# Arithmetic moved from GpSimd to VectorE, a hand-set order in the routing, and norms finished on the rows, in a two-block float32 layer kernel

## The chip, the cores and the metric

The kernel runs on one core of one Trainium2 chip. The metric is the device time of one execution in microseconds, from the first to the last instruction with what the launch adds around it; 1645.51 us is the median of three runs before the change. Five engines work side by side, each through its own fixed list of instructions: TensorE (PE, matmuls; PEld is its weight load), VectorE (DVE), ScalarE (ACT), GpSimd (POOL) and SyncE (SP), which here only issues DMAs.

## The reference

All is float32, for 256 tokens of width 1024 and 256 context tokens. Block one is a layer with a spatial gating branch, a tiny attention inside of it, a neighbourhood attention and a mixture of experts; block two has two layers of attention and a feed-forward part, with layer norms behind each.

```python
h   = modulate(rms_norm(x, g), shift, scale);  p_in = h @ w_in + b_in
u, v = gelu(...), gelu(...)                    # 1024 columns each
tq, tk = axial_rope(...), axial_rope(...)      # 64 columns each
vn  = layer_norm(v, ln_g, ln_b)
o_a = u * (w_s-mixed vn + b_s + tiny_attention(...) @ tiny_w_o)
o_b = neighbourhood_attention(nq, nk, nv, ..., rpb)
x   = x + g_mix * ((gate_a*(o_a@w_up_a) + gate_b*(o_b@w_up_b)) @ w_out)
h2  = modulate(rms_norm(x, g), shift, scale)
scores = sigmoid(h2 @ w_router); idx = top_k(scores + b_router, 8)   # of 64
x   = x + g_ffn * (sum over experts of swiglu * weight + shared swiglu)
x   = rms_norm(x, final_g)
for l in 0, 1:                                 # block two
    x = layer_norm(ALPHA*x + mixer(x), g, b)   # rope on part of q and k
    x = layer_norm(ALPHA*x + swiglu(x), g, b)
```

## The kernel before, in words

**Weights.** Every weight crosses the chip once, in pieces of 1 MB (128 x 2048). A ring of slots (`self.ring`) holds them: SyncE issues the next load when the slot of an older piece is released (`ring.done`). For full accuracy most products are made from split operands: `presplit` (L327 to 348) takes a piece, ScalarE casts it to the matmul's format (`whi`, L343), and VectorE subtracts that from the piece (`wlo`, L345). Each product is then three matmuls: high by high, low by high, high by low (L384 to 386, L476 to 478, L527 to 529). The pieces are cut in halves or quarters (`self.pieces`); while `pool_split` is set, in the first 60 us or so, every second quarter's subtraction goes to GpSimd. `split` (L287 to 289) does the same to activations.

**Order.** A planner (the Tile framework's scheduler) simulates the program with costs of its own and gives every engine a fixed list. An engine works through its list in order: an instruction that waits holds up all behind it. `issue_after` adds an order by hand.

**Block one, to 355 us.** The modulation rows, u, v and the queries and keys come from weight pieces in a row. The layer norm of v (L942 to 948) has its mean and scale on VectorE (L946), the gain `sg` and bias `sb` on GpSimd (L947, L948). `tiny` (L1150 and on) multiplies its queries and keys with cosine and sine on GpSimd (L1165 to 1170) into `ropet`, which TensorE transposes (L1177, L1179). The neighbourhood attention works in four groups of heads; for each, `load` (L1265 and on) fetches a bias tile T by two DMAs on GpSimd's queue and adds a mask to it on GpSimd (L1274); VectorE then adds T to the scores (L1289) and takes maxima. VectorE meanwhile sums gate rows (L737). `gate_bcast` spreads a gate row over the partitions with TensorE and ScalarE; `col_scale` (L324) multiplies the four pieces of `w_out` by it on GpSimd.

**Routing, 355 to 379 us.** x1 is normed and transposed (`x1_fm`, to_fm), split on GpSimd for the gathers (`xnh`, `xnl`, L1103 and L1104), and multiplied with the router (`logits`), the top 8 of 64 are found on VectorE (`top`), positions counted (`position`, `ranks`), while TensorE computes the shared expert's gate and up products (`shared`, one call for each half of the tokens). `gate_bcast(5)` follows.

**Experts, 379 to 850 us.** Twenty-six units of one, two or four experts; for each, the tokens are gathered by a matmul, and two weight stages and a scatter by a matmul follow (`gu` L1585, `down` L1624, `comb` L1637). 17 ring slots hold expert weights.

**Final norm and block two, 850 to 1645 us.** `final` takes the mean square, scales the rows by the inverse root (L1826 on ScalarE, L1828 on VectorE), and `next_x` transposes them (L1865): `to_fm` evacuates four 128x128 pieces with gain (and bias) per partition, two on ScalarE (L1873) and two on VectorE (L1870), into a tile `xf`; a cast (L1881) and a subtraction (L1882) give `xTh` and `xTl`, from which the first projection starts (L476). The rows themselves, `xr`, get the gain later (L1846). `layer_end` does the same behind each mixer and FFN of block two: mean and scale on the rows (L1916), gain and bias per partition behind the transposes, and on the rows later (L1944, L1945). The last norm of the kernel already finishes on the rows. `rope2` (L2101 to 2106) rotates part of q and k on GpSimd.

Of the kernel before, what the change touches and what calls it, by code (L numbers as in the profile page):

```python
# [18 lines left out]
D = 1024  # L19
# [252 lines left out]
class Kernel:  # L272
# [37 lines left out]

    def bcast_row(self, pool, tag, c0, n, eng=None):
# [248 lines left out]
    def program(self):  # L560
        tc, nc, A = self.tc, self.nc, self.A
        with ExitStack() as es:
# [58 lines left out]
            self.pool_split = False  # L621
            self.hfree = [self.hip] * self.HI
            self.hclosed = set()
            self.hlast = {}
# [145 lines left out]
    def block1(self):  # L770
# [102 lines left out]
        self.pieces, self.pool_split = 4, True  # L873
# [36 lines left out]
        self.pieces, self.pool_split = 2, False  # L910
# [131 lines left out]
        self.gate_bcast(2, gf)  # L1042
        self.route_tiles(self.adap.tile([128, D], F32, tag="gate2", name="route"), xp)
# [9 lines left out]
        for i in self.i_out:  # L1053
            self.col_scale(i, gf)
        for n, i in enumerate(self.i_upb):
# [63 lines left out]
        x1_fm(0)  # L1119
        logits(0)  # L1120
        self.shared(h2, 0)
        x1_fm(1)
        after = logits(1)
        top(0)
        top(1)
        last = position()
        self.shared(h2, 1)
        with tc.issue_after(after.ins):
            for t in range(2):
                self.shared_act(t)  # L1130
# [4 lines left out]
        mmes.close()  # L1135
        self.moe(xnh, xnl, gf, ranks, overflow)
# [12 lines left out]
    def tiny(self, ap, pool, t4, tT):  # L1149
# [10 lines left out]
        for s in range(2):  # L1160
# [4 lines left out]
            nc.gpsimd.tensor_tensor(o[:, :, :, 0], x1, cos, op=OP.mult)  # L1165
            nc.gpsimd.tensor_tensor(m[:, 0], x2, sin, op=OP.mult)
            nc.gpsimd.tensor_tensor(o[:, :, :, 0], o[:, :, :, 0], m[:, 0], op=OP.subtract)
            nc.gpsimd.tensor_tensor(o[:, :, :, 1], x2, cos, op=OP.mult)
            nc.gpsimd.tensor_tensor(m[:, 1], x1, sin, op=OP.mult)
            nc.gpsimd.tensor_tensor(o[:, :, :, 1], o[:, :, :, 1], m[:, 1], op=OP.add)  # L1170
# [79 lines left out]
    def na(self, ap, tmp, qd, kd, nv, obh, obl):  # L1250
# [15 lines left out]
        def load(g):  # L1266
# [7 lines left out]
            nc.gpsimd.tensor_tensor(t[:], t[:], m[:, ::-1, None].to_broadcast([128, 64, 24]), op=OP.add)  # L1274
# [80 lines left out]
    def routing(self, mix, h2):  # L1355
# [4 lines left out]
        def logits(t):  # L1360
            ps = self.mmp.tile([128, 512], F32, tag="mm", name="mm")
            for k in range(8):
                nc.tensor.matmul(ps[:, 0:64], h2[:, t, k], wr[:, k, :], start=k == 0, stop=k == 7)
            i = nc.scalar.activation(scs[:, t], ps[:, 0:64], AF.Sigmoid)
            if t == 1:
                return self.preload("silu_and_others", i)
# [15 lines left out]
        def position():  # L1382
# [8 lines left out]
            for t in range(2):  # L1391
                i = nc.tensor.matmul(ps[:, 192:256], self.onesb[:], mskb[:, t, 0], start=False, stop=t == 1, skip_group_check=True)
            for t in range(2):
                nc.vector.scalar_tensor_tensor(self.pw[:, t, 0], ps[:, t * 64:(t + 1) * 64], 1.0, msk[:, t], op0=OP.add, op1=OP.mult)

# [13 lines left out]
            return i  # L1409

        def ranks(pool, step):

            if step == 0:
# [72 lines left out]
    def shared(self, h2, t):  # L1486

        nc = self.nc
        ps = self.mmp.tile([128, 512], F32, tag="mm", name="shy")
        self.shp = getattr(self, "shp", []) + [ps]  # L1490
        for n in range(2):
            w = self.ring.get(self.i_sh[n])[:].rearrange("p (k c) -> p k c", k=8)
            for m in range(2):
                j = 2 * n + m
                for k in range(8):
                    nc.tensor.matmul(ps[:, j * 128:(j + 1) * 128], w[:, k, m * 128:(m + 1) * 128], h2[:, t, k],
                                     start=j == 0 and k == 0, stop=j == 3 and k == 7, skip_group_check=True)
            if t:
                self.ring.done(self.i_sh[n])

    def shared_act(self, t):
# [3 lines left out]
        ps = self.shp[t][:].rearrange("p (n m c) -> p n m c", n=2, m=2)  # L1505
# [4 lines left out]
    def moe(self, xnh, xnl, gf, ranks, overflow):  # L1510
# [5 lines left out]
        pg = es.enter_context(tc.tile_pool(name="pg", bufs=1, space=PSUM))  # L1516
# [4 lines left out]
        xgs = [self.hip.tile([128, 8, 256], F32, tag="hl", name="xg") for _ in range(2)]  # L1521
# [16 lines left out]
        def mkS(g):  # L1538
            S = mp.tile([128, 2, 2, 128], F32R, tag="S", name="S")
            for u in (2 * g, 2 * g + 1):  # L1540
                n, _ = UNITS[u]
                for t in range(2):
                    nc.vector.tensor_tensor(unit(S, u)[:, t], io1[:, None, 0:128 // n].to_broadcast([128, n, 128 // n]),
                                            table(u, 0)[:, t], op=OP.is_equal)
            st["S", g] = S
            st["xg", g] = xgs[g % 2]
# [7 lines left out]
        def gather(g, q):  # L1554
            S = st["S", g]
            xg = st["xg", g]
# [18 lines left out]
        def gu(p, k):  # L1575
            if k == 0:
                st["gu"] = pg.tile([128, 512], F32, tag="gu", name="gu")
            xg = st["xg", p // 2]
# [71 lines left out]
        mkS(0)  # L1650
# [7 lines left out]
        for p in range(nu):  # L1658
# [26 lines left out]
            if p == 1:  # L1685
                overflow(pg)
                shared_down()
        comb(nu - 2)
# [3 lines left out]
        self.overflow_loop(pg, xnh, xnl, [xgs[0][:].rearrange("p a b -> p (a b)"), wx[0][:], wx[1][:]], gf)  # L1692
# [29 lines left out]
    def ov_unit(self, pg, xnh, xnl, lst, wt, gf):  # L1722
# [3 lines left out]
        xg = self.xp.tile([128, 8, 64], F32, tag="x01", name="oxg")  # L1726
# [73 lines left out]
    def final(self, fp):  # L1800
# [15 lines left out]
        def a(t):  # L1816
# [6 lines left out]
            for h in range(2):  # L1823
                s = slice(h * 512, (h + 1) * 512)
                if h:
                    nc.scalar.activation(xn[:, t, s], self.acc[t][h][:], AF.Copy, scale=r[:])  # L1826
                else:
                    nc.vector.tensor_scalar(xn[:, t, s], self.acc[t][h][:], r[:], None, op0=OP.mult)  # L1828

        def b(t):  # L1830
            for h in range(2):
                i = self.next_x(xn[:, t, h * 512:(h + 1) * 512], t, h, self.vecs[:, V_FG:V_FG + 8], None, fp)
            return i
# [6 lines left out]
        i = self.weave_group(self.mixer_start(0), lambda: b(1))  # L1840
        self.pieces = 2
        with tc.issue_after(self.ring.last.ins):
            fg = self.bcast_row(fp, "fg", R_FG, 1024, nc.sync)
        with tc.issue_after(i.ins):
            for t in range(2):
                nc.vector.tensor_tensor(self.xr[:, t], self.xr[:, t], fg[:], op=OP.mult)  # L1846
        self.dump("x3", self.xr[:])

    def weave_group(self, steps, mid):
# [5 lines left out]
        i = mid()  # L1855
        for f in steps[0][n:]:
            f()
        return i
# [17 lines left out]
    def next_x(self, src, t, h, g, b, pool):  # L1876
# [484 lines left out]
```

## Time and profile before

| | us |
|---|---|
| three runs | 1643.67, 1645.51, 1646.34 |
| profiled execution | 1646.58 |
| its span | 1644.8 |
| mean granted TensorE clock | 0.981 |
| busy: PE, DVE, ACT, POOL | 1566.2, 894.2, 644.3, 133.9 |

The span is one execution, from its first to its last instruction; the execution's own time is 1.8 us longer. Busy times count an engine's work, not its waits; a share is of the span. The granted clock is the share of full speed (2.4 GHz) that TensorE had; its lower level, 1.2 GHz, is 0.5. A view by windows sums busy time in stretches of the span; a view of waits sums the idle time in front of an engine's instructions, by the instruction that waited and by what came last of what it waited for.

### The profile page before, as it was taken

To read this page: it belongs to the slowest core of one execution; us is meant where nothing else is said; L and a number is where in the kernel's file an instruction comes from. 1 tells how busy PE (TensorE), PEld (TensorE's weight loads), DVE (VectorE), ACT (ScalarE), POOL (GpSimd) and SP (SyncE) were. 2 spreads that over 40 slices of the span, in tenths; PEclk is the share of its full clock that TensorE was granted. 3 is DMA by queue.
4 is the path that set the end of the run, shared out by engine and by line. 5 is a ranking of instruction groups with operands and counts; after the bars stand their busy time and mean duration, and the time that the engine had idled before them with its cause. 6 is when DMAs were issued, how large, how long until landed. Compare 5 with 4: busy or idle time off the path is not lost. (4 is left out here: it accounts for less than half of the span.)

```text
span 1644.8 us, 26103 instructions
## 1 busy us (share of the span) xinstructions
PE 1566.2 (95%) x10517; PEld 1212.6 (74%) x10517; DVE 894.2 (54%) x1583; ACT 644.3 (39%) x1187; POOL 133.9 (8%) x128
## 2 busy tenths in 40 slices
PE   6998989899999999999979999999999999999997
PEld 4787778885444344433329999899999999889996
DVE  3696579854333233222344557965456565975454
ACT  3633367342122111111133656644343656644440
POOL 2234221511000000000000010000000010000000
PEclk9998999999999999999989999999999999999999
DMA  9779596776999999999974436555552444755540
GB/s 348 270 280 273 151 217 215 307 307 248 358 389 420 421 421 420 421 422 421 421 312 148 160 133 219 206 200 185 185 187 89 146 142 149 256 198 188 192 140 26
DMA packets 62586, 418.96 MB, mean 255 GB/s; under 512 B 7392, under 2 KB 9056, under 8 KB 13824
## 3 DMA queue, kind: packets, MB, share of 16 engines
q1 hardware_dynamic: 56304, 397.88, 63.7%
q0 software_dynamic: 3408, 15.84, 3.9%
q10 hardware_dynamic: 2752, 3.55, 0.6%
q8 instruction: 83, 1.36, 0.3%
q14 instruction: 39, 0.32, 0.1%
HBM read 413.05 MB, written 4.19 MB: 254 GB/s over the span
## 5 line engine op out<-in xcount | busy, mean ns | idle before, releaser
L345 DVE TENSOR_TENSOR wlo<-w,whi 128x1024 fp32r<-128x1024 f32 (+1 forms) x372 | 388.7, 1080 | 177.9 <-ACT whi L343 174.7
L343 ACT CAST whi<-w 128x1024 fp32r<-128x1024 f32 (+1 forms) x384 | 319.9, 882 | 319.1 <-PE mm L385 147.1
L384 PE MATMUL mm<-xTh,whi 128*128 128x256 f32 x960 | 274.5, 286 | 0.0
L386 PE MATMUL mm<-xTh,wlo 128*128 128x256 f32 x960 | 271.5, 283 | 0.0
L385 PE MATMUL mm<-xTl,whi 128*128 128x256 f32 x960 | 271.0, 282 | 0.0
L1585 PE MATMUL gu<-w,xg 128*64 128x512 f32 (+2 forms) x944 | 210.0, 604 | 2.4 <-DMA w<-in_we 2.4
L384 PEld LDWEIGHTS mm<-xTh,whi 128*128 128x128 f32 x960 | 182.9, 191 | 2.2 <-issue 1.4
L385 PEld LDWEIGHTS mm<-xTl,whi 128*128 128x128 f32 x960 | 183.4, 191 | 0.6
L386 PEld LDWEIGHTS mm<-xTh,wlo 128*128 128x128 f32 x960 | 182.8, 190 | 0.0
L1585 PEld LDWEIGHTS gu<-w,xg 128*64 128x64 f32 (+2 forms) x944 | 59.5, 128 | 111.3 <-issue 102.6
L1624 PE MATMUL y<-w,aT 128*64 128x512 f32 (+2 forms) x416 | 111.2, 599 | 0.0
L1606 DVE SCALAR_TENSOR_TENSOR sil<-sil,wsl,gu 128x256 f32<-128x256 f32 x26 | 12.5, 480 | 133.1 <-ACT sil L1605 132.5
L476 PE MATMUL acc<-whi,xTh 128*128 128x256 f32 x256 | 75.5, 295 | 7.3 <-ACT xTh L1881 7.3
L1704 ACT CAST yh<-yf 128x512 fp32r<-128x512 f32 x52 | 32.2, 619 | 125.8 <-DVE yf L1703 125.8
L385 PE MATMUL mm<-hl,whi 128*128 128x256 f32 x256 | 74.9, 293 | 4.6 <-DVE hl L289 4.6
L1703 DVE TENSOR_TENSOR yf<-y,gf 128x512 f32<-128x512 f32 x52 | 35.9, 690 | 78.0 <-PE y L1624 78.0
L384 PE MATMUL mm<-hh,whi 128*128 128x256 f32 x256 | 75.4, 297 | 1.5 <-ACT hh L288 1.5
L1624 PEld LDWEIGHTS y<-w,aT 128*64 128x64 f32 (+2 forms) x416 | 31.1, 126 | 61.7 <-issue 58.9
L386 PE MATMUL mm<-hh,wlo 128*128 128x256 f32 x256 | 74.8, 293 | 1.6 <-DVE wlo L345 1.6
L478 PE MATMUL acc<-whi,xTl 128*128 128x256 f32 x256 | 74.7, 293 | 0.0
L477 PE MATMUL acc<-wlo,xTh 128*128 128x256 f32 x256 | 74.5, 291 | 0.0
L1605 ACT ACTIVATE sil<-gu 128x256 f32<-128x256 f32 x26 | 10.0, 384 | 140.7 <-PE gu L1585 140.7
(460 smaller groups left out, 3271.3 us busy)
## 6 DMA issues: line engine op xcount, KB each, us to landing
w<-in_we SPq DMA_DIRECT2D x170, 1024.0 KB, 19.8
w<-in_w SPq DMA_DIRECT2D x157, 1024.0 KB, 4.9
w<-in_wada SPq DMA_DIRECT2D x23, 1024.0 KB, 8.8
wx<-in_we SPq DMA_DIRECT2D x22, 1024.0 KB, 19.8
ks<-kd POOLq DMA_DIRECT2D x8, 512.0 KB, 6.8
lngb<-in_rows POOLq DMA_DIRECT2D x4, 1024.0 KB, 5.7
T<-in_rpb POOLq DMA_DIRECT2D x8, 384.0 KB, 11.3
qs<-qd POOLq DMA_DIRECT2D x16, 128.0 KB, 6.6
```

The costliest lines, as they stand in the source:

```text
L343: nc.scalar.copy(hi[:, s], w[:, s])
L345: self.lo_of[i] = eng.tensor_tensor(lo[:, s], w[:, s], hi[:, s].bitcast(F32), op=OP.subtract)
L384: nc.tensor.matmul(ps, hi[:, k, mm], h, start=first, stop=False, skip_group_check=True)
L385: nc.tensor.matmul(ps, hi[:, k, mm], l, start=False, stop=False, skip_group_check=True)
L386: nc.tensor.matmul(ps, lo[:, k, mm], h, start=False, stop=last, skip_group_check=True)
L476: nc.tensor.matmul(o, h, wh, start=k == 0 and c % 2 == 0, stop=False, skip_group_check=True)
L477: nc.tensor.matmul(o, h, wl, start=False, stop=False, skip_group_check=True)
L478: nc.tensor.matmul(o, l, wh, start=False, stop=k == 7 and c % 2 == 1, skip_group_check=True)
L1585: nc.tensor.matmul(st["gu"][m * e:m * e + m, :], xg[:, k, s0:s0 + m], w[:, k % 4, :], start=k == 0, stop=k == 7, tile_position=(0, m * e))
L1624: nc.tensor.matmul(y[m * e:m * e + m, :], st["aT"][:, f * 128 + e * m:f * 128 + e * m + m], w[:, f, h * 512:(h + 1) * 512], start=f == 0, ...
L1703: nc.vector.tensor_tensor(t[0:n], y[0:n], g[0:n, h * 512:(h + 1) * 512], op=OP.mult)
L1704: nc.scalar.copy(yh[0:n], t[0:n])
```

## The change

- **GpSimd to VectorE:** the early weight splits (`pool_split` goes), the gain and bias of v's layer norm, tiny's rope, T's mask, block two's rope, and the split of x1 (`x1_split`: the copy on VectorE for the first half of the tokens and on ScalarE for the second, the subtraction on VectorE). `col_scale` stays on GpSimd, and so do its DMAs and the memsets.
- **gate_bcast(5)** moves in front of the gated products, works in place, and one DMA on GpSimd's queue copies it to `gf` behind the column scalings.
- **Routing:** `follow` makes every matmul of a passage follow the one before it. The steps of `logits` and `shared` are lists; one shared product follows each logits product, the rest stand in front of `top`, `position` and the gather. The second part of `position` becomes `keys`, called behind the first table of the gather. The shared expert's products for the second half of the tokens go into the first expert unit, and the second gather tile is allocated behind them.
- **Final norm:** the gain is loaded by two DMAs on GpSimd's queue late in the expert stage and applied on the rows by VectorE.
- **Layer norms of block two:** gain and bias on the rows, in front of the transposes; the later multiplications and additions go.
- **next_x** splits straight from PSUM, in pieces of 256 columns.

```diff
@@ presplit
-                eng = nc.gpsimd if self.pool_split and h % 2 else nc.vector
-                self.lo_of[i] = eng.tensor_tensor(lo[:, s], w[:, s], hi[:, s].bitcast(F32), op=OP.subtract)
+                self.lo_of[i] = nc.vector.tensor_tensor(lo[:, s], w[:, s], hi[:, s].bitcast(F32), op=OP.subtract)
@@ layer norm of v
-            nc.gpsimd.tensor_tensor(v[:, t], v[:, t], sg[:], op=OP.mult)
-            nc.gpsimd.tensor_tensor(v[:, t], v[:, t], sb[:], op=OP.add)
+            nc.vector.tensor_tensor(v[:, t], v[:, t], sg[:], op=OP.mult)
+            nc.vector.tensor_tensor(v[:, t], v[:, t], sb[:], op=OP.add)
@@ gated products
         self.gate_bcast(2, gf)
+        self.gate_bcast(5, self.gate_row[5])
...
             self.col_scale(i, gf)
+        nc.gpsimd.dma_start(gf[:], self.gate_row[5][:])
@@ x1
+        def x1_split(t):
             for h in range(2):
                 s = slice(h * 512, (h + 1) * 512)
-                nc.gpsimd.tensor_copy(xnh[:, t, s], xn2[t][h][:])
-                nc.gpsimd.tensor_tensor(xnl[:, t, s], xn2[t][h][:], xnh[:, t, s].bitcast(F32), op=OP.subtract)
+                if t:
+                    nc.scalar.copy(xnh[:, t, s], xn2[t][h][:])
+                else:
+                    nc.vector.tensor_copy(xnh[:, t, s], xn2[t][h][:])
+                nc.vector.tensor_tensor(xnl[:, t, s], xn2[t][h][:], xnh[:, t, s].bitcast(F32), op=OP.subtract)
@@ routing
+        with self.follow():
+            x1_fm(0)
+        x1_split(0)
+        sh = iter(self.shared(h2, 0, self.mmp))
...
+        for t in range(2):
+            for f in logits(t):
+                with self.follow():
+                    f()
+                    more(1)
+            if t == 0:
+                with self.follow():
+                    x1_fm(1)
+                ends = [self.last(e) for e in (mybir.EngineType.Activation, mybir.EngineType.DVE)]
+                with self.follow():
+                    more(4)
+        after = self.sigmoid
+        with tc.issue_after(ends[0]), tc.issue_after(ends[1]):
+            x1_split(1)
+            top(0)
         top(1)
-        last = position()
-        self.shared(h2, 1)
...
-        with tc.issue_after(last.ins):
-            self.gate_bcast(5, gf)
+        with self.follow():
+            more(7)
+        with self.follow():
+            position()
+        with self.follow():
+            more(5)
@@ tiny (six such lines), T's mask, rope2 (six such lines)
-            nc.gpsimd.tensor_tensor(o[:, :, :, 0], x1, cos, op=OP.mult)
+            nc.vector.tensor_tensor(o[:, :, :, 0], x1, cos, op=OP.mult)
...
-            nc.gpsimd.tensor_tensor(t[:], t[:], m[:, ::-1, None].to_broadcast([128, 64, 24]), op=OP.add)
+            nc.vector.tensor_tensor(t[:], t[:], m[:, ::-1, None].to_broadcast([128, 64, 24]), op=OP.add)
@@ moe
+        i = mkS(0)
+        ranks(None, -1)
+        with tc.issue_after(after.ins), tc.issue_after(i.ins):
+            self.shared_act(0)
...
                     trS(p)
+                    if p == 0:
+                        for f in self.shared(h2, 1, pg):
+                            f()
+                        self.shared_act(1)
+                        xgs.append(self.hip.tile([128, 8, 256], F32, tag="hl", name="xg"))
...
+        for h in range(2):
+            t = self.xp.tile([128, 512], F32, tag=("x01", "x00")[h], name="fg")
+            r = A["rows"]
+            nc.gpsimd.dma_start(t[:], bass.AP(tensor=r.tensor, offset=r.offset + R_FG + h * 512, ap=[[0, 128], [1, 512]]))
+            self.fg.append(t)
@@ final
-                if h:
-                    nc.scalar.activation(xn[:, t, s], self.acc[t][h][:], AF.Copy, scale=r[:])
-                else:
-                    nc.vector.tensor_scalar(xn[:, t, s], self.acc[t][h][:], r[:], None, op0=OP.mult)
+                nc.vector.scalar_tensor_tensor(xn[:, t, s], self.acc[t][h][:], r[:], self.fg[h][:], op0=OP.mult, op1=OP.mult)
...
-                nc.vector.tensor_tensor(self.xr[:, t], self.xr[:, t], fg[:], op=OP.mult)
@@ next_x
-        xf = pool.tile([128, 4, 128], F32, tag="xf", name="xf", bufs=2)
-        self.to_fm(src, h, g, b, xf, 4 * h)
-        nc.scalar.copy(self.xTh[:, t, ks], xf[:])
-        return nc.vector.tensor_tensor(self.xTl[:, t, ks], xf[:], self.xTh[:, t, ks].bitcast(F32), op=OP.subtract)
+        ps = self.mmp.tile([128, 512], F32, tag="mm", name="mm")
+        for k in range(4):
+            nc.tensor.transpose(ps[:, k * 128:(k + 1) * 128], src[:, k * 128:(k + 1) * 128], self.ident)
+        for p in range(2):
+            ks = slice(4 * h + 2 * p, 4 * h + 2 * p + 2)
+            self.split(ps[:, p * 256:(p + 1) * 256].rearrange("p (k c) -> p k c", k=2), self.xTh[:, t, ks], self.xTl[:, t, ks])
@@ layer_end (the last norm had this form already)
             for s in hs:
+                nc.vector.scalar_tensor_tensor(y[:, s], y[:, s], mv[:, 0:1], gb[:, s], op0=OP.subtract, op1=OP.mult)
+                nc.vector.scalar_tensor_tensor(y[:, s], y[:, s], r[:], gb[:, D + s.start:D + s.stop], op0=OP.mult, op1=OP.add)
...
-                nc.vector.tensor_tensor(self.xr[:, t], self.xr[:, t], gb[:, 0:D], op=OP.mult)
-                nc.vector.tensor_tensor(self.xr[:, t], self.xr[:, t], gb[:, D:2 * D], op=OP.add)
```

## Rows read from the trace of the kernel before

**Rows 1.** Busy us, share of the span and instructions of each engine.
```profile
PE 1566.2 (95%) x10517; PEld 1212.6 (74%) x10517; DVE 894.2 (54%) x1583; ACT 644.3 (39%) x1187; POOL 133.9 (8%) x128
```

**Rows 2.** Stretches of the span: busy us and instructions, granted clock, DMA share, GB/s.
```profile
140.00:155.00 15.00, 8.91 (x52) 8.03 (x50) 7.86 (x7) 1.54 (x3) 13.71 (x19) 0.66 0.95 254
...
189.00:240.00 51.00, 43.20 (x387) 37.73 (x386) 40.07 (x60) 27.81 (x64) 17.32 (x21) 1.00 0.68 175
...
480.00:735.00 255.00, 253.78 (x1298) 109.50 (x1294) 80.25 (x171) 45.77 (x102) 0.00 (x0) 1.00 1.01 421
...
1050.00:1065.00 15.00, 11.70 (x69) 10.45 (x68) 14.67 (x38) 8.63 (x16) 0.00 (x0) 0.89 0.61 223
```
The five busy columns are PE, PEld, DVE, ACT and POOL.

**Rows 3.** Waits of PE: us in total, times, longest.
```profile
PE mm L1865 <- DVE xr L1828: 8.1, 2, 7.3
PE acc L476 <- ACT xTh L1881: 7.3, 3, 3.3
...
PE acc L1280 <- ACT P L1234: 5.1, 1, 5.1
PE mm L385 <- DVE hl L289: 4.6, 4, 2.1
PE acc L1177 <- POOL ropet L1170: 3.3, 1, 3.3
PE acc L1179 <- POOL ropet L1170: 2.8, 1, 2.8
...
PE gu L1585 <- DMA w<-in_we: 2.4, 2, 1.4
PE mm L420 <- DVE wlo L345: 2.0, 1, 2.0
```

**Rows 4.** POOL by line: count, busy us, mean ns, idle us before and its releaser.
```profile
L345 POOL TENSOR_TENSOR wlo<-w,whi 128x512 fp32r<-128x512 f32 x12 | 17.6, 1487 | 41.6 <-ACT whi L343 41.6
L1274 POOL TENSOR_TENSOR T<-T,catt 128x1536 f32<-128x1536 f32 x4 | 11.4, 2840 | 24.2 <-DMA T<-in_rpb 24.2
...
L948 POOL TENSOR_TENSOR v<-v,sb 128x1024 f32<-128x1024 f32 x2 | 6.7, 3384 | 0.0
...
L1165 POOL TENSOR_TENSOR ropet<-tt__720,catt 128x64 f32<-128x64 f32 x2 | 2.7, 1339 | 0.0
```

**Rows 5.** DVE by line and shape, over the whole span, columns as in rows 4.
```profile
L737 DVE SCALAR_TENSOR_TENSOR gate<-w,silp,gate 128x1024 f32<-128x1024 f32 x30 | 47.5, 1582 | 0.4
L289 DVE TENSOR_TENSOR al<-s,ah 128x256 fp32r<-128x256 f32 x36 | 13.6, 418 | 0.1
...
L1892 DVE SCALAR_TENSOR_TENSOR xr<-xr,acc 128x512 f32<-128x512 f32 x16 | 10.7, 681 | 17.8 <-PE acc L529 17.8
...
L1944 DVE TENSOR_TENSOR xr<-xr,lngb 128x1024 f32<-128x1024 f32 x6 | 7.1, 1218 | 0.0
...
L1380 DVE TENSOR_SCALAR pw<-pw,winv 128x64 f32<-128x64 f32 x2 | 0.5, 254 | 0.0
```

**Rows 6.** DVE by line and shape, from 100 to 120 us.
```profile
L737 DVE SCALAR_TENSOR_TENSOR gate<-w,silp,gate 128x1024 f32<-128x1024 f32 x5 | 14.0, 2791 | 0.1
```

**Rows 7.** PE's timeline, start and us: first and last of 22 matmuls.
```profile
149.85 0.56 PE L419 MATMUL mm<-whi,ch 128*128 128x256 f32 x1
...
154.47 0.32 PE L419 MATMUL mm<-whi,ch 128*128 128x256 f32 x1
```

**Rows 8.** Timeline of all engines behind the first mixer's norm.
```profile
1052.92 1.00 DVE L1916 TENSOR_SCALAR xr<-xr,lmv,rs_y 128x512 f32<-128x512 f32 x2
...
1057.47 1.15 ACT L1881 CAST xTh<-xf 128x512 fp32r<-128x512 f32 x2
...
1058.15 0.39 PE L476 MATMUL acc<-whi,xTh 128*128 128x256 f32 x1 [3.31 <-ACT xTh L1881]
```

**Rows 9.** Timeline of all engines behind the final norm.
```profile
857.74 1.97 PE L1865 MATMUL mm<-cst,xr 128*128 128x128 f32 x8 [7.33 <-DVE xr L1828]
...
863.08 0.58 PE L476 MATMUL acc<-whi,xTh 128*128 128x256 f32 x1 [0.64 <-ACT xTh L1881]
```

More of the change, by code (lines that the diff above doesn't have):

```diff
@@ L1 @@
 import math
-from contextlib import ExitStack
+from contextlib import ExitStack, contextmanager
 import numpy as np
@@ L309, in rsqrt, with follow, last @@
         return y
+    @contextmanager
+    def follow(self):
+        traced = self.nc.cur_bb.bb.instructions
+        n = len(traced)
+        with self.tc.issue_after(self.pe_last) if self.pe_last else ExitStack():
+            yield
+        for i in traced[n:]:
+            if i.engine == mybir.EngineType.PE:
+                self.pe_last = i
+    def last(self, engine):
+        return next(i for i in reversed(self.nc.cur_bb.bb.instructions) if i.engine == engine)
     def bcast_row(self, pool, tag, c0, n, eng=None):
@@ L872, in block1 @@
             f()
-        self.pieces, self.pool_split = 4, True
+        self.pieces = 4
         self.presplit()
@@ L909, in block1 @@
             f()
-        self.pieces, self.pool_split = 2, False
+        self.pieces = 2
         self.setup3()
@@ L1118, in block1, with more @@
         x1(1)
[L1119 to L1124, printed above, removed]
-        top(1)
-        last = position()
-        self.shared(h2, 1)
-        with tc.issue_after(after.ins):
-            for t in range(2):
-                self.shared_act(t)
-        with tc.issue_after(last.ins):
-            self.gate_bcast(5, gf)
+        with self.follow():
+            x1_fm(0)
+        x1_split(0)
+        sh = iter(self.shared(h2, 0, self.mmp))
+        def more(n):
+            for _ in range(n):
+                next(sh)()
+        for t in range(2):
[13 more added lines that the diff above has]
+            top(0)
+        top(1)
+        with self.follow():
[4 more added lines that the diff above has]
+            more(5)
         self.dump("h2", h2[:])
         adap_es.close()
-        mmes.close()
-        self.moe(xnh, xnl, gf, ranks, overflow)
+        self.moe(xnh, xnl, gf, h2, after, mmes, ranks, overflow)
         ext3_es.close()
@@ L1360, in logits, with step @@
         def logits(t):
[L1361 to L1366, printed above, removed]
+            def step(k):
+                if k == 0:
+                    st["ps"] = self.mmp.tile([128, 512], F32, tag="mm", name="mm")
+                ps = st["ps"][:, 0:64]
+                nc.tensor.matmul(ps, h2[:, t, k], wr[:, k, :], start=k == 0, stop=k == 7)
+                if k == 7:
+                    self.sigmoid = nc.scalar.activation(scs[:, t], ps, AF.Sigmoid)
+                    if t == 1:
+                        self.sigmoid = self.preload("silu_and_others", self.sigmoid)
+            return [lambda k=k: step(k) for k in range(8)]
         def top(t):
@@ L1484, in bank, with shared, step @@
         return pool.tile([128, 512], F32, tag="bank", name=name, bufs=3)
-    def shared(self, h2, t):
+    def shared(self, h2, t, pool):
         nc = self.nc
-        ps = self.mmp.tile([128, 512], F32, tag="mm", name="shy")
-        self.shp = getattr(self, "shp", []) + [ps]
-        for n in range(2):
+        ps = self.bank(pool, "shy") if t else pool.tile([128, 512], F32, tag="mm", name="shy")
+        self.shp = ps
+        def step(n, m, k):
             w = self.ring.get(self.i_sh[n])[:].rearrange("p (k c) -> p k c", k=8)
[L1493 to L1498, printed above, removed]
+            j = 2 * n + m
+            nc.tensor.matmul(ps[:, j * 128:(j + 1) * 128], w[:, k, m * 128:(m + 1) * 128], h2[:, t, k],
+                             start=j == 0 and k == 0, stop=j == 3 and k == 7, skip_group_check=True)
+            if t and m and k == 7:
                 self.ring.done(self.i_sh[n])
+        return [lambda n=n, m=m, k=k: step(n, m, k) for n in range(2) for m in range(2) for k in range(8)]
     def shared_act(self, t):
@@ L1520, in moe @@
         nu = len(UNITS)
-        xgs = [self.hip.tile([128, 8, 256], F32, tag="hl", name="xg") for _ in range(2)]
+        xgs = [self.hip.tile([128, 8, 256], F32, tag="hl", name="xg")]
         wx = []
@@ L1725, in ov_unit @@
         op = self.mp
-        xg = self.xp.tile([128, 8, 64], F32, tag="x01", name="oxg")
+        xg = wt[3]
         tmpf = op.tile([128, 256], F32, tag="sil", name="otmp")[:, 0:128].rearrange("p (a b) -> p a b", a=2)
@@ L1839, in final @@
         self.open_hlx(0)
-        i = self.weave_group(self.mixer_start(0), lambda: b(1))
+        self.weave_group(self.mixer_start(0), lambda: b(1))
         self.pieces = 2
[L1842 to L1845, printed above, removed]
-                nc.vector.tensor_tensor(self.xr[:, t], self.xr[:, t], fg[:], op=OP.mult)
         self.dump("x3", self.xr[:])
```

79 lines of the change are left out of this document (35 added, 44 removed).

## The prediction, made before the change was run

> **What bounds the kernel now.** I began with the busy shares: TensorE works 95% of the span, and no other engine comes near [rows 1]. So time can come only from TensorE's idle time, from the clock it loses, or from work taken off it; the change takes no arithmetic off it. The stretches come next. In the expert stage TensorE is busy 253.78 of 255 us while the DMA rings move 421 GB/s, so two limits lie on each other there; before and after it the engine idles in small holes, 7.8 us of it in the 51 us of windowed attention, and its granted clock drops in some stretches: 0.66 on average at 140 to 155, 0.89 at 1050 to 1065 [rows 2]. That is a mixture of the two levels, 2.4 and 1.2 GHz, and it shows where holes are long. The waits of TensorE then say who ends each hole [rows 3]: the rows that the change can reach are the two on ropet, one each on wlo (L420) and hl, the two in front of block 2 on xr and xTh, and a small one on expert weights. They are all a few microseconds long, so the sum is one of small terms.
>
> **The change, part by part.** It is made against the profiled execution: 1646.6 us, of which the span is 1644.8; the median shown is 1645.5, 1.1 less.
>
> *Tiny rope.* GpSimd's twelve small products (1.3 us each for the multiplications, [rows 4]) become VectorE's at about 0.25 (the nearest VectorE row of 64 columns [rows 5], 0.15 to 0.5 as bounds): 3 us in all. TensorE's two waits of 3.3 and 2.8 [rows 3] should go, since the products are then done before it gets there, and with them the low clock behind them: the 22 matmuls from 149.85 to 154.47 take 4.6 us at the lower level [rows 7]; at the upper one half of that would do, so some 2. Together **-8** (if VectorE's order puts the products behind three gate products of 1.6 each [rows 5], 3 of it remain: -8 to -3).
>
> *Layer norm of v.* Four GpSimd instructions of 3.4 us [rows 4] become four of 1.22 on VectorE (the 128x1024 product with a row, [rows 5]): +4.9 there. In the same 20 us VectorE's gate products took 2.79 each, five of them [rows 6], against 1.34 for the other 25 (47.5 less 14.0, over 25, [rows 5, 6]): 7.2 us come back. VectorE is 2.3 better off, and the one wait on wlo of 2.0 [rows 3] ends earlier: **-2.4** (-3 to +2, the upper end if the four sit in front of a split that TensorE needs).
>
> *Early weight splits.* Twelve subtractions of 1.49 us [rows 4] join VectorE at 0.68 (a 128x512 product, [rows 5]): +8.2, about what it loses beside GpSimd in that stretch now. The waits on hl there are 4.6 [rows 3]; a second engine is gone, but so is the slow piece of each weight. **-2** (-4 to +2).
>
> *Mask added to the bias T.* Four of 2.84 us [rows 4] become four of 1.83 on VectorE (1.5 times 1.22, [rows 5]): 7.3, in a stretch in which VectorE is busy 40 of 51 us and feeds the softmax [rows 2]. By the gates' contention (2.79 less 1.34, [rows 5, 6]) something like 2 us come back; half of the remaining 5.3 falls into VectorE's own gaps. **+3**. What hangs on it is order: an engine runs its list in order, and the addition can't start before T's DMA has landed. GpSimd waited 24.2 us for that in all [rows 4], with nothing behind it but DMA issues; behind VectorE's additions stand the additions of T to the scores, the maxima and the weight splits. If all of it lands on the path it is 24.2 + 7.3 = 31.5; below, 7.3 - 11.4 = -4, if VectorE regains all that GpSimd's additions last. I take the low value because the DMAs that bring T are no longer queued behind GpSimd's arithmetic, and because an order that is planned ahead places the addition late in VectorE's list if it expects the transfer to be slow.
>
> The Trainium skill ("SBUF — State Buffer", section "SBUF: two separate sides") says that a GpSimd instruction and a VectorE instruction with two SBUF inputs hold their shared port pair as an exclusive lock for the whole instruction, the other one waiting. The trace shows the two slowing each other (1.34 to 2.79), but by less than the 3.4 us that a whole GpSimd instruction lasts [rows 4 to 6]. By the rule, VectorE would get back every microsecond of GpSimd's; that result stands as a rival below.
>
> *x1 split, gate_bcast(5), routing.* The order of TensorE's work between 355 and 381 is fixed by hand: logits between the shared expert's products, and the half of the shared expert for tokens 128 to 255 goes behind the first gathers; gate_bcast goes forward, its result kept in place and copied by a DMA on GpSimd's queue behind the four column scalings (the scalings stay on GpSimd). Nothing is dropped, and the engine is dense on both sides (253.78 of 255, [rows 2]), so a matmul moved from one dense stretch to another is worth nothing; the earlier gather is paid for by the later shared products. **0** (-2 to +2, where the two weight slots of the shared expert, freed later, start 2 MB of expert weights up to 2 / 0.421 = 4.8 us later, if the ring were empty; it isn't at that moment). The split of x1 (three subtractions and copies per half, 0.7 each) is off TensorE's path until the gather.
>
> *Final norm.* The gain is now applied on the rows, and comes by two DMAs of 256 KB inside the saturated stage: 0.5 MB at 421 GB/s [rows 2] is 1.2 us, taken as **+0.5** (0 to 1.2). Between the first transposes of the normed rows, 857.74, and the first projection, 863.08, lie 5.3 us [rows 9]: transposes, four scaled evacuations, a cast over 512, and the second tile's eight transposes (1.97 at the low clock, [rows 9]). Now two 256-wide casts follow the four transposes at once (0.42, the 256-wide subtraction, [rows 5]), so 1.0 + 0.2 + 0.4 + 1.97 = 3.6 remain; the clock comes back somewhat earlier. **-2.5** (-5 to +1, the second half of the rows being on VectorE now).
>
> *Two mixer norms.* Each has one hole of 3.31 us in front of the first gate product: rows ready from 1052.92, cast at 1057.47, first matmul 1058.15 [rows 8]; the final norm's 0.6 makes the 7.3 of the waits [rows 3]. Two instructions of 0.5 per tile become four of 0.68 [rows 5, 8]: the first half of the rows is 0.9 later, the second 1.7. Against that, transposes, one 256-wide cast (0.42) and the first matmul follow directly, and four k tiles can run while the second half comes. I count holes of 0.5, 0.6 and 0.6, 1.7 instead of 3.3, -1.6; none is as long as 3 us, so the clock (0.89 over 11.7 busy us, 1.3, [rows 2]) should stay: **-3 each, -6** (each -5 to +1, the upper end if the 1.7 is paid in full and the pieces queue behind weight splits). The multiplications and additions after the norm, twelve of 1.22 [rows 5], vanish from VectorE, off the path. The FFN's norm shows no such hole: 0.
>
> *Block 2's rope.* 24 products move to VectorE, 24 x 0.25 = 6 us where it has room: **-0.5** (-1 to +3).
>
> Sum: -8 -2.4 -2 +3 +0 +0.5 -2.5 -6 -0.5 = -17.9: 1628.7 for an execution like the profiled one, 1.1 less beside the median: **1627.6**, say 1628.
>
> **Rivals.** *Front given back*: the weights come too late for the time gained. For it: a wait of 5.1 on P [rows 3] came from ScalarE sitting in front of a weight DMA that hadn't landed; it would simply be met earlier. Against: TensorE, not the rings, is nearly full in most of the front. Price: the -12.4 of the first three terms vanish: 1640. *VectorE blocked by T* (slower): its four additions stand at the head of VectorE's queue until T lands, 31.5 instead of +3: 1656. It decides once more than 13 of the 24.2 us [rows 4] ahead of the four additions reach TensorE (7.3 + 13.6 = 20.9, what the other terms give). *Everything comes back*: VectorE regains the whole of each GpSimd instruction; T then gives 4 instead of costing 3: 1621. The lock that the Trainium skill ("SBUF — State Buffer", section "SBUF: two separate sides") describes would do this; by the contention that the gates show it is less. *Earlier experts*: the gather, some microseconds earlier, frees ring slots earlier, and the 2.4 us of waits on expert weights [rows 3] and the clock behind them go: 4 less, 1624. *It doesn't do all it says*: rope's products stay behind the gates on VectorE, -3 instead of -8, 1633; that lies within the forecast's own range.
>
> **How the numbers follow.** A measurement of this kernel tells a difference of some 0.2% (3.3 us) from none. Chances: forecast 0.47 (own range 1617 to 1637), front given back 0.20, blocked by T 0.15, everything back 0.08, earlier experts 0.10. Blocked by T is nearly all of slower, 0.14; of front given back, whose 1640 lies 5.5 below the median, and of the milder blockings, 0.10 fall within 0.2%; faster 0.76. The range, 1611 to 1648, leaves out most of the blocked case and 0.06 below.
>
> **What would show it.** The two waits on ropet gone and the clock at 140 to 155 near 1; no VectorE idle time ended by T's DMA above a few microseconds (over 13, and the forecast is wrong); the wait on xTh in front of the mixer's gate product below 1.5 each with the clock above 0.95 there; the expert stage as long as before; the gap before block 2's first projection some 2.5 shorter. A longer wait on expert weights, or on P behind ScalarE, would name the rivals.

## The result, and the profile after

The changed kernel takes 1626.8 us (median of four, 1625.5 to 1627.0) against 1645.9 before: ratio 0.9883, 95% interval 0.9865 to 0.9902. The forecast was 1628. The time was met partly by luck: the loss in the windowed attention was put some 9 us too small, and the gains together some 12 us too small, and the two errors cancelled. Both are taken apart here.

The busy shares of the kernel after, to be held against [rows 1]:
```profile
PE 1565.1 (96%) x10517; PEld 1211.2 (75%) x10517; DVE 888.1 (55%) x1629; ACT 632.1 (39%) x1171; POOL 58.6 (4%) x67
```
TensorE's work is the same (1565 against 1566) in a span of 1625.2 instead of 1644.8; GpSimd has lost 75 us. So 18.5 of the span's 19.6 us are TensorE's idle time (78.6 before, 60.1 after).

TensorE's waits after (total, times, longest), for [rows 3]:
```profile
...
PE mm L397 <- ACT whi L357: 10.7, 3, 6.0
PE mm L399 <- DVE wlo L358: 7.1, 6, 2.5
PE mm L1935 <- DVE xr L1889: 4.4, 1, 4.4
PE acc L1343 <- ACT P L1271: 2.6, 1, 2.6
...
PE gu L1633 <- DMA wx<-in_we: 2.5, 2, 1.4
PE gu L1633 <- DMA w<-in_we: 1.9, 2, 1.4
```
Gone: both waits on ropet, all but 0.4 of the 4.6 on hl, and the 7.3 on xTh in front of block two's products. New: 10.7 us for weight casts by ScalarE, of which 10.2 fall in the windowed attention. The waits on expert weights grew, from 2.9 in the kernel before (2.4 on w and 0.5 on wx) to 4.4, so the rival "earlier experts" falls.

Stretches after, columns as in [rows 2]: projections with the rope, most of the attention, experts, first mixer norm.
```profile
125.00:150.00 25.00, 25.00 (x194) 23.21 (x194) 19.56 (x22) 9.50 (x15) 4.92 (x10) 1.00 1.10 287
...
190.00:285.00 95.00, 80.88 (x741) 70.23 (x741) 76.99 (x109) 59.54 (x134) 12.91 (x25) 0.91 0.70 208
470.00:730.00 260.00, 258.20 (x1316) 110.82 (x1314) 82.93 (x176) 47.00 (x104) 0.00 (x0) 1.00 1.01 421
1038.00:1053.00 15.00, 15.00 (x103) 13.44 (x102) 14.92 (x36) 9.08 (x18) 0.00 (x0) 1.00 0.60 211
```
TensorE is fully busy at full clock around the rope (clock 0.66 before) and around the mixer's norm (11.7 of 15 us and 0.89 before); in the attention it idles 14 of 95 us and its clock is 0.91.

The clearest view is a ledger: the start of the same matmul in both traces, and how the lead grows.

| TensorE reaches | before | after | lead | step |
|---|---|---|---|---|
| context projections | 101.8 | 97.2 | 4.7 | early splits: -4.7 |
| context values | 128.1 | 120.5 | 7.6 | v's norm: -2.9 |
| last projection | 164.2 | 147.5 | 16.7 | rope: -9.1 |
| last gate column | 207.9 | 190.7 | 17.2 | -0.6 |
| end of attention | 289.6 | 284.6 | 5.0 | +12.2 |
| x1's transposes | 354.9 | 352.0 | 2.9 | +2.1 |
| first gather | 379.2 | 366.4 | 12.8 | (work moved) |
| overflow count, after the first expert units | 409.0 | 403.4 | 5.6 | routing: -2.7 |
| last scatter | 849.5 | 845.5 | 4.0 | +1.6 |
| second weight group of block two | 888.3 | 878.2 | 10.1 | final norm: -6.1 |
| first FFN's down products | 1084.4 | 1069.5 | 14.9 | rope2 -0.4, mixer norm -4.4 |
| second FFN | 1474.6 | 1454.8 | 19.7 | -0.7, mixer norm -4.1 |
| end of span | 1644.8 | 1625.2 | 19.7 | 0 |

Over half of what the front gained by 165 us is lost again between 208 and 290. In the attention's stretch TensorE's idle time grows by 6.3 us (7.9 to 14.1), the clock's loss by 4.0, and 1.9 us are gate_bcast(5), moved there and given back in the routing; together that is the 12.2 of the ledger.

The mixer's norm after, timeline (for [rows 8]):
```profile
1042.47 1.41 DVE L1968 SCALAR_TENSOR_TENSOR xr<-xr,rs_y,lngb 128x512 f32<-128x512 f32 x2
1043.31 1.28 PE L1935 MATMUL mm<-cst,xr 128*128 128x128 f32 x8
...
1043.97 0.37 ACT L288 CAST xTh<-mm 128x256 fp32r<-128x256 f32 x1 [1.31 <-PE mm L1935]
1044.39 0.39 PE L489 MATMUL acc<-whi,xTh 128*128 128x256 f32 x1
```
From the first transposes to the first product it is 1.1 us (1043.31 to 1044.39); before it was 4.3 (1053.81 to 1058.15). No hole is left. The rows' first pass doesn't even stand in this chain: it needs only the mean, and runs while the inverse root is computed; so of the 1.7 us that I had put on the rows 0.4 stand on the path (1.41 instead of 1.0).

The final norm after (for [rows 9]):
```profile
849.95 1.41 DVE L1889 SCALAR_TENSOR_TENSOR xr<-acc,rs_y,fg 128x512 f32<-128x512 f32 x2
850.75 1.97 PE L1935 MATMUL mm<-cst,xr 128*128 128x128 f32 x8 [4.37 <-DVE xr L1889]
...
852.37 0.56 PE L489 MATMUL acc<-whi,xTh 128*128 128x256 f32 x1
```
The wait on the rows fell from 7.3 to 4.4. Of these 3.0 us, 1.7 are VectorE's: from the first sum of squares to the first scaled row it takes 1.9 us (848.03 to 849.95) instead of 3.6 (853.32 to 856.93), since no weight split stands between the steps of the first root any more. The other 1.3 are ScalarE's: its squares begin 0.3 us behind the last scatter (846.39 to 846.73), before it was 1.6 (850.40 to 852.02), with three weight casts in front of them that end only at 850.37; that these casts held them isn't shown. The first product follows 1.6 us behind the transposes, not 5.3, as the second tile's transposes now come after it.

### The profile page after: what moved, and what is told of

It reads as the page before. It is cut to its first block, busy times and chain, and to the rows that moved or that the text cites. A ratio compares the mean times of both kernels' runs of the same rounds, so it can differ in the third digit from the quotient of the medians.

```text
span 1625.2 us, 26035 instructions
## 1 busy us (share of the span) xinstructions
PE 1565.1 (96%) x10517; PEld 1211.2 (75%) x10517; DVE 888.1 (55%) x1629; ACT 632.1 (39%) x1171; POOL 58.6 (4%) x67
## 5 line engine op out<-in xcount | busy, mean ns | idle before, releaser
L1633 PE MATMUL gu<-w,xg 128*64 128x512 f32 (+2 forms) x896 | 200.9, 597 | 1.9 <-DMA w<-in_we 1.9
L1672 PE MATMUL y<-w,aT 128*64 128x512 f32 (+2 forms) x464 | 121.9, 599 | 0.0
L397 PE MATMUL mm<-hh,whi 128*128 128x256 f32 x256 | 76.7, 302 | 12.3 <-ACT whi L357 10.7
L1672 PEld LDWEIGHTS y<-w,aT 128*64 128x64 f32 (+2 forms) x464 | 35.7, 126 | 62.4 <-issue 59.0
L1767 DVE TENSOR_TENSOR yf<-y,gf 128x512 f32<-128x512 f32 x52 | 35.9, 690 | 78.6 <-PE y L1672 78.6
## 6 DMA issues: line engine op xcount, KB each, us to landing
w<-in_wada SPq DMA_DIRECT2D x23, 1024.0 KB, 10.2
```

Of the source, the lines that this page charges most:

```text
L397: nc.tensor.matmul(ps, hi[:, k, mm], h, start=first, stop=False, skip_group_check=True)
L1633: nc.tensor.matmul(st["gu"][m * e:m * e + m, :], xg[:, k, s0:s0 + m], w[:, k % 4, :], start=k == 0, stop=k == 7, tile_position=(0, m * e))
L1672: nc.tensor.matmul(y[m * e:m * e + m, :], st["aT"][:, f * 128 + e * m:f * 128 + e * m + m], w[:, f, h * 512:(h + 1) * 512], start=f == 0, ...
L1767: nc.vector.tensor_tensor(t[0:n], y[0:n], g[0:n, h * 512:(h + 1) * 512], op=OP.mult)
```

## The experiments

**Four parts alone, on the kernel before.** `p_gp` has only the GpSimd arithmetic moved (x1's split left), `p_ln` only the norms, `p_route` only the routing with gate_bcast and x1's split, `p_rope` only the tiny rope. Their edits are the corresponding pieces of the diff.

> The kernel before with the GpSimd arithmetic alone on VectorE (early splits, v's gain and bias, both ropes, T's mask). Theory W (the front's gains wait for weights: the windowed attention is paced by 1 MB pieces that come through few ring slots beside the bursts of T, q and k): TensorE is 15 to 17 us ahead at the end of the projections, as with the whole change, and 2 to 5 us ahead when the gated products start; in all 3 to 6 us faster, about 1640 to 1643. Theory V (what is lost in the attention is VectorE's four additions of T): the same sum here, but TensorE's holes there end with VectorE's work on scores, not with weight casts behind a DMA. If the loss in the attention comes from another part of the change, this kernel keeps 15 us: about 1630.

> The kernel before with tiny's twelve rope products alone on VectorE. All theories: the two waits on ropet go and the low clock behind them, so TensorE is 8 to 9 us ahead at 165 us. Theory W: the windowed attention gives 5 to 9 of it back through weights that land no earlier, 0 to 4 us faster in all (1641.5 to 1645.5), with longer holes behind weight casts. Theory V: nothing is given back, since T stays on GpSimd: 8 to 9 us faster, about 1637.

> The kernel before with the norms alone changed: final norm with its gain on the rows, layer norms of block two finished on the rows, tokens split from PSUM. From the whole change's trace: 6.1 us at the final norm, 4.4 and 4.1 at the two mixer norms, some 0.5 at the FFN's norm: 14 to 15 us faster, about 1631, if the parts are independent. If the final norm's 6.1 came in part from the expert stage ending in another order, 11 to 12: 1634. By the prediction's terms (2.5 and twice 3, less 0.5): 8, about 1637.5.

> The kernel before with the routing's order alone (x1's split off GpSimd, gate_bcast forward, shared products fixed and half of them behind the first gathers). Theory C (matmuls moved between dense stretches cost nothing): gather some 9 to 10 us earlier, the shared products' 7.2 and the gate's 1.9 paid elsewhere, so within 2 us of before, 1643.5 to 1646.5. Theory E (an earlier gather shortens the expert stage): 4 to 7 us faster, 1639 to 1641.5.

| kernel | ratio to before | span against before's profile, us |
|---|---|---|
| p_gp | 0.9935 (0.9917 to 0.9952) | -7.4 |
| p_rope | 0.9957 (0.9937 to 0.9978) | -3.0 |
| p_ln | 0.9909 (0.9876 to 0.9943) | -13.2 |
| p_route | 1.0016 (0.9995 to 1.0037) | +2.1 |

The kernel before spread from 1640 to 1655 here, so the ratios are to be read with their intervals. The spans of the three disjoint parts (p_rope is a part of p_gp) add up to -18.5, near the whole's -19.7. p_ln gave what the trace of the whole said (5.8 at the final norm, 4.4 and 4.2 at the mixers, 1.3 lost in the expert stage where its DMAs are). p_route gained nothing: the gather came 5.5 us earlier and the overflow count 1.7 later. It isn't the routing alone, though: the lists in front of it moved as well, and it was 4.5 us ahead at the last gate column and 4.4 behind at x1's transposes. From there to the overflow count it gained 2.7, as the whole change did. p_gp was 15.6 us ahead at the last projection, as theory W said, and 7.0 in front of x1, more than W's 2 to 5. p_rope won 9.1 at the rope, after 2 lost just ahead of it, and came out of the attention with 3.5, although T was on GpSimd there: so some give-back (3.6 us) is independent of T's mask, and theory V, alone, falls. The rope's ratio allows 3.6 to 10.4 us, so that its own amount isn't settled.

The waits of p_gp from 100 to 355 us show what holds TensorE there, weight casts and not VectorE's work on the scores:
```profile
PE mm L383 <- ACT whi L343: 9.9, 2, 5.8
PE acc L503 <- ACT whi L343: 6.4, 1, 6.4
```

**Undoing T's mask, and taking T's transfers away, on the changed kernel.**
```diff
# a_tpool
-            nc.vector.tensor_tensor(t[:], t[:], m[:, ::-1, None]...
+            nc.gpsimd.tensor_tensor(t[:], t[:], m[:, ::-1, None]...
# a_noT
-            for rl in range(2):
+            if g:
+                nc.gpsimd.memset(t[:], 0.0)
+            for rl in range(0 if g else 2):
                 nc.gpsimd.dma_start(
```


> The changed kernel with T's mask back on GpSimd, all else as changed. Theory V (the attention's loss is VectorE's four additions of T, 7.0 us in a busy stretch): the attention from the last gate column to its last output matmul, 94.0 us in the changed kernel, is 5 to 7 shorter, about 1620 to 1622. Theory W (its pace is set by weight pieces that land late): within 2 us of the changed kernel, 1625 to 1629, and TensorE still waits about 10 us for weight casts there.

> The changed kernel without the transfers of the bias tiles of groups 1 to 3 (their tiles are set to zero on GpSimd instead, so the bias of these heads is left out); VectorE's additions stay. Theory W1 (the weights land late because T's bursts share the rings with them; one took 12.7 us): TensorE's 10.2 us of waits for weight casts in the attention fall below 5, and the clock's loss behind them with it: 1618 to 1621. Theory W2 (the weight's load is issued too late, since its ring slot comes free late): waits of 6 or more stay, 1624 to 1627.

a_tpool: 1619.3, ratio 0.9834 (0.9791 to 0.9878), span 1616.4, TensorE's waits for casts in the attention 1.2 instead of 10.2. a_noT, which leaves the bias out for three of the four groups of heads: 1619.1, ratio 0.9821 (0.9775 to 0.9866), span 1617.9, those waits 4.3:
```profile
PE mm L397 <- ACT whi L357: 4.3, 2, 2.2
```
Each reaches its own theory's number: a_tpool V's (0.7 below the range), a_noT W1's. VectorE has the same additions in a_noT, so their 7.0 us of work aren't the cause by themselves. And a_tpool takes away more than VectorE's work: the planner gave the stage another order (in the changed kernel the gate columns run to 190.7 and the next weight's products start behind them, at 190.8; there those start at 187.1, and the gate columns run to 195.2). What both change is when the weights come. The loads of the ring by SyncE in the changed kernel:
```profile
176.52 0.33 SPq L222 DMA_DIRECT2D w<-in_w  x1
199.92 0.33 SPq L222 DMA_DIRECT2D w<-in_wada  x1
204.27 0.33 SPq L222 DMA_DIRECT2D w<-in_w  x1
```
The cast of that last weight stood at the head of ScalarE's list:
```profile
216.95 1.99 ACT L357 CAST whi<-w 128x1024 fp32r<-128x1024 f32 x2 [6.31 <-DMA w<-in_w]
```
The weight took 12.7 us to land. Without T's transfers the same load, issued at 204.20, was there at 213.06, after 8.9:
```profile
213.06 1.99 ACT L357 CAST whi<-w 128x1024 fp32r<-128x1024 f32 x2 [2.50 <-DMA w<-in_w]
```
T's transfers aren't all that it shared the queues with. What was moved from 204.27 to 216.93 in the changed kernel, packets and MB by queue (q1 is SyncE's, q0 GpSimd's):
```profile
q1 hardware_dynamic: 367, 2.74, 72.4%
q0 software_dynamic: 234, 0.97, 31.8%
```
The load's own 1.05 MB are the smaller part of the 2.74; the rest are the gate pieces loaded in front of it and behind it. In a_noT the two are 2.35 and 0.25 MB in its 8.9 us. With T's mask on GpSimd the ring moves earlier instead:
```profile
177.97 0.33 SPq L222 DMA_DIRECT2D w<-in_w  x1
182.01 0.33 SPq L222 DMA_DIRECT2D w<-in_wada  x1
194.43 0.33 SPq L222 DMA_DIRECT2D w<-in_w  x1
```
(these three are of its second run, a_tpool2, below): the gate piece is loaded 18 us earlier, the weight behind it 10. In a_tpool that weight, issued at 196.82, had the queues nearly to itself and landed after 4.8. The two sums of an older gate piece, which free a slot of the ring, stand in front of the first scores in VectorE's list there (they end at 183.13, the load starts at 183.16), and behind them in the changed kernel (204.24; the weight's load starts at 204.27). The scores begin 5.6 us earlier in the changed kernel (183.9, not 189.5), though their T is masked later (by 182.3 on VectorE, by 176.8 on GpSimd): it is the list that differs, and why the planner chose it isn't shown.

**The order of the ring, and the list.**
```diff
# a_ada
-    ADA_AFTER = {8: 1, 10: 2, ..., 14: 1, ..., 19: 1, 20: 1, 21: 1}
+    ADA_AFTER = {8: 1, 9: 1, 10: 2, ..., 14: 2, ..., 19: 1}
# a_gate
-            for j, f in enumerate(along(15 + n)):
+            for j, f in enumerate(along(15) + along(16) if n == 0 else along(16 + n)):
```


> The changed kernel with two of the seven gate-weight pieces that lie between the attention's weight pieces moved forward in the ring's order (one behind the first query piece, one behind the last value piece). Theory W2 (weights stand behind gate pieces in a ring of few slots): two holes behind weight casts go or halve, 3 to 8 us faster, 1619 to 1624. Theory W1 or V: nothing, or a loss where VectorE's gate sums now fall into the projections: 1626 to 1631.

> The changed kernel with the gate sums of the attention handed to the planner one weight earlier, so that VectorE's list has the third piece's two sums some six places earlier among the score work; T's additions stay on VectorE, T's transfers as they are. Theory O (a gate sum that stands behind the scores frees its ring slot late, so the next weight is loaded late): the 23 us in which the ring's next load waits around 176 to 200 shorten, the waits for weight casts fall below 6, 4 to 8 us faster than the changed kernel. Theory V (VectorE's 7 us of additions): no change, within 2 us. Theory W1 (transfers alone): at most 3 us faster.

> The changed kernel once more, beside the next three on one chip. All theories: ratio to the kernel before 0.986 to 0.991, as at first, and TensorE waits twice, some 10 us, for weight casts in the attention.

> T's mask back on GpSimd once more, beside the changed kernel on one chip: by its first profile 8.8 us less span; all theories 7 to 10 us faster than the changed kernel, some 1618, if that profile was no accident.

> Both: T's mask on GpSimd and the gate sums one weight earlier. Theory O: T on GpSimd has already put the gate sums in front of the scores, so the second edit adds little, within 3 us of T on GpSimd alone. Theory V: the same time as T on GpSimd alone, since only VectorE's load counts. If order and load are separate costs, 4 or more us faster than T on GpSimd alone.

a_ada: 1625.8, 0.987 (0.9824 to 0.9916): no gain; of the casts' waits half went (5.0), and 4.1 us of idle came in front of the spatial gating's products, at 165. The last four on one chip:

| kernel | us | ratio to before |
|---|---|---|
| a_again (the change) | 1625.1 | 0.9870 (0.9855 to 0.9885) |
| a_gate | 1634.4 | 0.9929 (0.9916 to 0.9943) |
| a_tpool2 | 1619.0 | 0.9832 (0.9813 to 0.9852) |
| a_both | 1625.7 | 0.9869 (0.9853 to 0.9885) |

a_gate missed in both directions: 9.3 us slower. The ring's longest wait stayed (22.7 us, now behind a gate sum), TensorE's waits for casts shrank to 1.9, and two of 8.8 and 8.5 behind ScalarE took their place, where ScalarE sat 18.9 us in front of weights that hadn't landed. So the edit didn't make the state that theory O speaks of, and O isn't tested by it; what it shows is that the same work in another order of the lists moves this stage by 9 us. a_both, 6.8 slower than a_tpool2, which no theory had, says the same. T's mask on GpSimd is the faster place twice: its run is 6.2 us below the change on the same chip, and it beats both kernels.

TensorE's waits in the attention of a_tpool2, 190 to 290 us:
```profile
PE acc L1317 <- ACT PT L1285: 3.4, 1, 3.4
PE mm L397 <- ACT whi L357: 1.5, 1, 1.5
```

**Split through a tile, on the changed kernel.** The rows stay as changed; the transposed tokens are first copied out of PSUM in four pieces.
```diff
# a_xf, next_x
+        for k in range(4):
+            if k % 2:
+                nc.vector.tensor_copy(xf[:, k], ps[:, k * 128:(k + 1) * 128])
+            else:
+                nc.scalar.copy(xf[:, k], ps[:, k * 128:(k + 1) * 128])
...
+        self.split(xf[:], self.xTh[:, t, ks], self.xTl[:, t, ks])
```


> The changed kernel with the norms still finished on the rows, but the transposed tokens first evacuated by four copies (two on ScalarE, two on VectorE) into an own tile and split from there in one cast and one subtraction over 512, as before. If the split straight from PSUM is what closes the holes in front of block two's first products, they come back, longer by the 1.7 of the rows' instructions: 2 to 4 us at the final norm and 4 to 6 at each mixer norm, 10 to 16 us slower, 1637 to 1643. If the rows' order alone did it (gain and bias out of the evacuations), within 3 us of the changed kernel.

1635.6, 0.9923 (0.99 to 0.9946); its span is 11.3 longer than the change's: 2.9 at the final norm, 3.9 at each mixer norm. The holes return:
```profile
PE acc L489 <- ACT xTh L288: 6.6, 3, 2.4
```
So the split straight from PSUM in two pieces (the run takes back both at once, and can't part them) is 3.9 of the 4.4 and 4.1 us at the mixers, and half of the 6.1 at the final norm; the other half there is the rows coming earlier.

## Why the prediction was right, and where it was not

- **Rope** (-8): -9.1; VectorE's products take 0.22 us, and the clock stayed up. **Norm of v** (-2.4): -2.9; the gate products beside it fell from 2.79 [rows 6] to 1.28:
```profile
L750 DVE SCALAR_TENSOR_TENSOR gate<-w,silp,gate 128x1024 f32<-128x1024 f32 x6 | 7.7, 1280 | 0.1
```
- **Early splits** (-2): -4.7, past the bound of -4; all of the 4.6 on hl went but 0.4.
- **T's mask** (+3): the step that was mis-sized, with the wrong mechanism. The additions were priced rightly, four of 1.75 (1.83 predicted), and VectorE never waited for T's transfer:
```profile
L1311 DVE TENSOR_TENSOR T<-T,catt 128x1536 f32<-128x1536 f32 x4 | 7.0, 1752 | 0.0
```
The zero is the idle time in front. The rival "VectorE blocked by T" thus fell at its first condition. But the stage lost 12.2 (10.3 without the gate's matmuls) and 2.1 more up to x1. Putting T's mask back on GpSimd, with the other order that came with it, gives back 6.2 of it by the medians. The rival "front given back" named the mechanism that ran: casts at the head of ScalarE's list behind weights that land late. It was priced at 12.4, near the mark, but as an alternative to the sum, not a part of it. The 2 us that were to come back from the contention were right: beside T's four masks one VectorE instruction was held in the kernel before, a gate product, 3.25 us instead of 1.27:
```profile
196.35 2.79 POOL L1274 TENSOR_TENSOR T<-T,catt 128x1536 f32<-128x1536 f32 x1 [3.81 <-DMA T<-in_rpb]
...
196.98 3.25 DVE L737 SCALAR_TENSOR_TENSOR gate<-w,silp,gate 128x1024 f32<-128x1024 f32 x1
```
- **Routing** (0): -2.7, of which 1.9 are the gate's matmuls coming back; right.
- **Gain's DMAs** (+0.5): +1.6 in the expert stage with the change, 1.3 in p_ln, none in p_gp and p_route (0.1 and -0.2). Above the bound of 1.2 by little.
- **Final norm** (-2.5): -6.1, below the bound of -5. I had left the rows' own delay as it was, and counted the second tile's transposes in front of the first product.
- **Mixer norms** (-6): -8.5. I had priced two of the rows' four instructions into the chain that ran beside the root, and three holes that didn't come.
- **Block two's rope** (-0.5): -0.4 in the first layer.

The losses (the attention and the gain's DMAs) were some 10 us larger than forecast and the gains some 12: the time was met, the sum wasn't, and that the two cancelled is luck.

Open stays how the loss in the attention divides between T's transfers at one time with k's and q's, the ring's own loads coming close together behind the slot that comes free late, and VectorE's load: taking away the first, or moving the addition, each brings most of it back, so they don't add; and the one edit meant to isolate the list's order made another order. Each edit of the attention also let the planner set other lists (a_noT has those of the changed kernel up to 211 us, behind the issue of the weight compared above), so that no such run's whole time shows one thing alone.

## What to carry to other kernels

A gain ahead of a stage that is fed by a few buffers can be lost in that stage, as 10.3 of 17.2 us were here: follow the lead over the whole program by the start of equal instructions, and price each later stage's refill. Work moved to the faster engine also moves everything that was planned around it; a slow engine that nothing waits for, as GpSimd for T, may be the better place. Where the layout allows, finish a value ahead of the transposes, and split from PSUM in small pieces: the first product then starts behind the first piece.

## What the runs showed of the hardware

GpSimd and VectorE could hold each other up for whole instructions. In a_tpool:
```profile
172.92 1.23 DVE L358 TENSOR_TENSOR wlo<-w,whi 128x1024 fp32r<-128x1024 f32 x1 [1.13 <-ACT whi L357]
173.29 3.50 POOL L1311 TENSOR_TENSOR T<-T,catt 128x1536 f32<-128x1536 f32 x1 [11.98 <-DMA T<-in_rpb]
...
174.39 3.48 DVE L358 TENSOR_TENSOR wlo<-w,whi 128x1024 fp32r<-128x1024 f32 x1
```
The subtraction of 1.22 us that began at 174.39 ended at 177.87, 1.1 behind the end of GpSimd's addition (176.79); the addition itself, 2.8 when alone, is 0.7 longer, and the subtraction before it ran 0.9 us into it (to 174.15). That is the exclusive lock that the Trainium skill states ("SBUF — State Buffer", section "SBUF: two separate sides"), and I had weighed it too low, taking means for durations. Not every instruction was held: in the same run the additions of T to the scores, which lie in PSUM, and the maxima took their usual 0.65 and 0.68 us beside GpSimd's additions (197.51 to 199.93, beside one from 196.44 to 199.44). So the rule's rival (1621), which gave VectorE back all 11.4 us of T's masks, doesn't follow: in the kernel before they had cost it 2.0.

The largest case is still in the changed kernel. The column scalings of `w_out` stayed on GpSimd, and beside them VectorE's weight subtractions, 1.2 us each when alone, take 2.5 to 5.7:
```profile
292.53 21.18 POOL L338 TENSOR_TENSOR w<-w,gf 128x2048 f32<-128x2048 f32 x4 [14.73 <-DMA w<-in_w]
295.69 8.12 DVE L358 TENSOR_TENSOR wlo<-w,whi 128x1024 fp32r<-128x1024 f32 x2 [0.21 <-ACT whi L357]
...
304.39 10.41 DVE L358 TENSOR_TENSOR wlo<-w,whi 128x1024 fp32r<-128x1024 f32 x2
```
The four scalings end at 297.15, 302.72, 308.24 and 313.71, and the four subtractions 1.1 us behind each (298.24, 303.80, 309.32, 314.79). That makes 13.8 us more for VectorE, and TensorE waits for the last two of them; its waits from 284 to 352 us:
```profile
PE mm L399 <- DVE wlo L358: 5.2, 3, 2.5
```
It was 5.4 there before. The change moved small products whose price was a few us and left this one; no run shows what moving it would bring.
